# The first projection stage of a short-convolution layer: one written order on all engines in place of the scheduler's

## The chip, the cores and the metric

The kernel runs on one core of a Trainium2 chip. The metric is the device time of one execution in microseconds. Before the change the median of three runs is 918.4 us (918.34 to 922.01). The profiled execution, to which all times of the trace belong, took 920.8 us, with a span of 919.0 us from its first to its last instruction.

In the profile PE is TensorE's matmul, PEld its weight load, DVE is VectorE, ACT is ScalarE, SP is the engine that issues nearly all loads. Each engine takes its instructions in the order in which the program has them.

## The reference

One layer is computed (batch 1, T = 256 positions, model width D = 2048, branch width E = 4096), all in float32:

```python
h = rmsnorm(x, norm_g)
mod = silu(c) @ ada_w + ada_b                # (1, 3*D)
shift, scale, gate = split(mod, 3)
h = h * (1 + scale) + shift                  # 256 x 2048
b_gate, c_gate, v, g = split(h @ w_in, 4)    # w_in: 2048 x 16384, four quarters of 4096
u = causal_depthwise_conv(c_gate * v, conv_w)        # three taps
y = b_gate * u * silu(g)
x = x + gate * (y @ w_out)                   # w_out: 4096 x 2048
out = rmsnorm(x, final_g)
```

## The kernel before, in words

**Products.** Weights and features are float32 and are split into a high part (rounded to the matmul's format) and a low part (the rest). Each product of a 128x128 piece of weights with 256 positions is three matmuls: high by high, high by low, low by high. A load of weights is a block of 128 x 2048 floats (1 MB, tile `raw_s`). ACT casts it into `hi` (line 347), DVE subtracts and writes `lo` (line 348); each of `raw`, `hi` and `lo` has three buffers. Making the two is called parting a block.

**Stages.** After an opening (norm, first features) comes the first w_in stage, whose results are the tiles `mm_s` in PSUM: 16 of the 32 column tiles of every quarter, in four channels of four tiles (names: `acc21` is channel 2, quarter 1). It is done while adaLN's shift and scale are still being summed: of the 16 rows of tiles of w_in (k) only two have features at its start, and more come in pairs. So the stage is done in passes. A pass takes one quarter and one or two channels over those k that have features by then, each channel in a PSUM bank of its own (three exist, tag "mm"). At its end the bank is copied into an accumulator by ACT (line 517, `keep`), or added to it by DVE (line 519); or the bank was seeded with the accumulator beforehand by ACT (line 533) and is only copied out. A bank's share of one block is 24 matmuls. Then the second w_in stage (`mm_b`, the other 16 column tiles) and the last product (`mm_o`) follow.

**adaLN.** A piece is two loads of 128 x 512 floats (tile `at`, 256 KB each, four buffers); DVE multiplies by silu(c) and adds up into `gv` (lines 455 and 457), two instructions a piece. Eight pieces give a pair of k. Then PE transposes (`tp_g`), ACT sums along rows, DVE makes scale and shift (lines 331 to 333), and ACT and DVE write the high and low halves of the pair's features into `hT` (lines 339 to 341). The sums for the residual gate (`at_g`, `gacc`, line 625) belong to the second stage, and the scheduler moves them up into the first where it sees room.

**Mixing.** When a channel has all four quarters, `mixed` multiplies two accumulators (line 570), takes SiLU (571), runs the three-tap filter (ACT line 418, DVE lines 419 and 422), multiplies twice (574, 575), and casts into `y` on ACT (427) and DVE (428), for two column tiles at a time.

**What sets the order.** `plan()` lists the passes, with the pieces to be loaded between blocks and whether a bank is seeded, by a small clock of its own. The program is then written pass by pass, and the framework's scheduler orders each engine's instructions by priority and estimated times; tiles get their buffers in that scheduled order. Three devices hold it: `in_order()` chains all instructions of the opening, `load` chains the first ten loads on SP, `behind` chains the first parts, and `later(GIVE)` puts the sums of adaLN far back in priority. `PACE` says how many pieces go with each of the first ten blocks.

Of the kernel before, what the change touches and what calls it, by code (L numbers as in the profile page):

```python
# [47 lines left out]
WAHEAD = 14.0  # L48
AAHEAD = 6.0


SHARE = 1.5
PACE = (0, 0, 2, 1, 2, 1, 2, 1, 2, 2)


def plan():
# [78 lines left out]
def short_conv_layer(ctx: ExitStack, tc: tile.TileContext, x, c, norm_g, ada_w, ada_b, w_in, conv_w, w_out, final_g, out):  # L135
# [20 lines left out]
    def raw_tile(name):  # L156
        return wpool.tile([P, SLOT], F32, tag="raw", name=name, bufs=3)
# [250 lines left out]
    for k in range(NK0):  # L408
# [1 line left out]
        nc.scalar.copy(hi0[:, c], raw0[:, c])  # L410
        nc.vector.tensor_tensor(out=lo0[:, c], in0=raw0[:, c], in1=hi0[:, c].bitcast(F32), op=ALU.subtract)
        features(k, sh_sc[:, k, 1:2], sh_sc[:, k, 0:1])
    pinned.close()
    pieces0 = [(hi0, lo0)]

    def conv(ct, u, cv):

        nc.scalar.activation(u, cv, AF.Copy, scale=cw[:, 64 + ct : 65 + ct])
        nc.vector.scalar_tensor_tensor(  # L419
            out=u[:, 1:T], in0=cv[:, 0 : T - 1], scalar=cw[:, 32 + ct : 33 + ct], in1=u[:, 1:T], op0=ALU.mult, op1=ALU.add  # L420
        )
        nc.vector.scalar_tensor_tensor(  # L422
            out=u[:, 2:T], in0=cv[:, 0 : T - 2], scalar=cw[:, ct : ct + 1], in1=u[:, 2:T], op0=ALU.mult, op1=ALU.add
        )

    def split_y(dst, y):
        nc.scalar.copy(dst[:, :, 0, :], y)
# [3 lines left out]
    acc = {}  # L431
    sums = {}

    def ada_piece(k0, nk, piece):
        w = nk * P
        kk = ASLOT // (2 * w)
        if piece == 0:
            sums[k0] = adap.tile([P, 2, 2 * P], F32, tag="gv", name="gv")
        gv = sums[k0][:, :, 0:w]
        j = piece * kk  # L440
        at = adap.tile([P, ASLOT], F32, tag="at", name="at", bufs=4)
        at4 = at.rearrange("p (k s f) -> p k s f", k=kk, s=2)
        for s in range(2):
            load(at4[:, :, s, :], adas[:, j : j + kk, s, k0 * P : k0 * P + w])
# [5 lines left out]
    def ada_sums(j, kk, at4, gv):  # L450
        for i in range(kk):
            c_k = silu_c[:, j + i : j + i + 1]
            with behind(ended if first_pieces or j + i == 0 else {}):
                if j + i == 0:
                    nc.vector.tensor_scalar_mul(gv, at4[:, i], c_k)
                else:
                    nc.vector.scalar_tensor_tensor(out=gv, in0=at4[:, i], scalar=c_k, in1=gv, op0=ALU.mult, op1=ALU.add)  # L457

    def ada_done(k0, nk, gv):

        tp = psum.tile([P, 4, P], F32, tag="sm", name="tp_g", bufs=2)
        gs = const.tile([P, 4], F32, tag="gs", name="gs", bufs=2)
        for o in range(2 * nk):
            nc.tensor.transpose(tp[:, o, :], gv[:, o // nk, (o % nk) * P : (o % nk + 1) * P], ident)  # L464
        for o in range(2 * nk):
            nc.scalar.activation(tp[:, o, :], tp[:, o, :], AF.Copy, accum_out=gs[:, o : o + 1])
        modulate(k0, nk, (gs[:, 0:nk], gs[:, nk : 2 * nk]))

    opener = [None]
    first_loads = [None] * 10  # L470

    def load(dst, src):

        ins = nc.sync.dma_start(dst, src)
        if first_loads:
            sp = ins.ins.engine
            tc.add_manual_dep(ins.ins, ended[sp], after, reason="in order")
            ended[sp] = ins.ins.name
            first_loads.pop()

    def product(dst, hi, lo, k, i, begins, left, ends):

        w, h = ((hi, hh_), (hi, hl_), (lo, hh_))[i]
# [34 lines left out]
        else:  # L518
            nc.vector.tensor_tensor(out=acc[ch, q], in0=bank, in1=acc[ch, q], op=ALU.add)

    first_pieces = [None] * 4

    def parts(chs, q, k0, k1, seeds, between):

        w = len(chs) * CT * P
        col = q * E + chs[0] * CT * P
        step = SLOT // w
        first = k0
        banks = []
        for ch, seed in zip(chs, seeds):  # L530
            banks.append(psum.tile([P, CT, T], F32, tag="mm", name="mm_s"))
            if seed:
                nc.scalar.copy(banks[-1], acc[ch, q])
        if pieces0:
            for k in range(NK0):
                chunk_products(banks[0], *pieces0[0], k * CT * P, k, k0, k1, late=True)
            pieces0.clear()
            k0 = NK0
            for some in between:
                for piece in some:  # L540
                    ada_piece(*piece)
        for s0, some in zip(range(k0, k1, step), between):
            sk = min(step, k1 - s0)
            n = sk * w
            raw = raw_tile("raw_s")
            load(
                raw[:, :n].rearrange("p (k f) -> p k f", k=sk),
                w_in[0, s0 * P : (s0 + sk) * P, col : col + w].rearrange("(k p) f -> p k f", p=P),
            )
            with behind(ended if first_pieces else {}, advance=True):  # L550
                hi, lo = split(raw, n)
            del first_pieces[:1]
            for piece in some:
                ada_piece(*piece)
            for j, (bank, seed) in enumerate(zip(banks, seeds)):
                if first == 0:
                    opening_products(bank, hi, lo, w, j * CT * P, s0, sk, k1)
                else:
                    for i in range(sk):
                        chunk_products(bank, hi, lo, i * w + j * CT * P, s0 + i, first, k1, seed)  # L560
        for ch, bank, seed in zip(chs, banks, seeds):
            keep(ch, q, first, bank, seed)

    ys = []

    def mixed(ch):

        for h in range(0, CT, 2):
            cq, vq, gq, bq = (acc[ch, q][:, h : h + 2, :] for q in QUARTERS)
            nc.vector.tensor_tensor(out=cq, in0=cq, in1=vq, op=ALU.mult)  # L570
            nc.scalar.activation(gq, gq, AF.Silu)
            for j in range(2):
                conv(ch * CT + h + j, vq[:, j, :], cq[:, j, :])
            nc.vector.tensor_tensor(out=gq, in0=gq, in1=bq, op=ALU.mult)
            nc.vector.tensor_tensor(out=vq, in0=vq, in1=gq, op=ALU.mult)
            ys.append(slot([P, 2, 2, T], f"y{len(ys)}", F32R))
            split_y(ys[-1], vq)

    whole = [0] * NCH
    for before, *step in plan():  # L580
        for piece in before:
            ada_piece(*piece)
        chs, k1 = step[0], step[3]
        parts(*step)
        for ch in chs:
            whole[ch] += k1 == KT
            if k1 == KT and whole[ch] == 4:
                mixed(ch)
# [208 lines left out]
```

## Time and profile before

| what | value |
|---|---|
| median of three runs | 918.4 us |
| profiled execution | 920.8 us |
| its span | 919.0 us |
| opening, to the first matmul of mm_s | 25.2 us |
| first stage (mm_s) | 25.2 to 388.6 us |
| second stage (mm_b) | 388.6 to 737.3 us |
| last product and end | 737.3 to 919.0 us |

The page's first part gives busy time and share by engine; a busy PE row is modelled at the ends. The chain of waits has the start, the length and the name of each piece of the chain that ended last. A group row ends with the idle time ahead of the group and who ended it. A windows row has the length, the busy time of PE, PEld, DVE, ACT and POOL with the number of instructions, then the granted TensorE clock, the busy share of the DMA engines and their GB/s. A timeline row has start and length, then what and how many, and in brackets the idle time before it.

### The profile page before, as it was taken

To read this page: it belongs to the slowest core of one execution; us is meant where nothing else is said; L and a number is where in the kernel's file an instruction comes from. 1 tells how busy PE (TensorE), PEld (TensorE's weight loads), DVE (VectorE), ACT (ScalarE), POOL (GpSimd) and SP (SyncE) were. 2 spreads that over 40 slices of the span, in tenths; PEclk is the share of its full clock that TensorE was granted. 3 is DMA by queue.
4 is the path that set the end of the run, shared out by engine and by line. 5 is a ranking of instruction groups with operands and counts; after the bars stand their busy time and mean duration, and the time that the engine had idled before them with its cause. 6 is when DMAs were issued, how large, how long until landed. Compare 5 with 4: busy or idle time off the path is not lost.

```text
span 919.0 us, 16211 instructions
## 1 busy us (share of the span) xinstructions
PE 898.6 (98%) x7041; PEld 859.8 (94%) x7041; DVE 629.6 (69%) x603; ACT 453.9 (49%) x431; POOL 2.3 (0%) x9
## 2 busy tenths in 40 slices
PE   7899999999999999999999999999999999999996
PEld 4899999999999999999999999999999988888885
DVE  5698999999886999875545554555454544545882
ACT  6677876554545665543344334433344333443333
POOL 1000000000000000000000000000000000000000
PEclk9999999999999999999999999999999999999999
DMA  9999999999898678676666656666666495566542
GB/s 308 364 375 374 335 358 363 335 375 343 299 322 288 219 275 295 206 243 193 186 196 201 197 184 192 198 203 188 185 191 197 142 356 212 191 204 200 183 137 92
DMA packets 146775, 227.64 MB, mean 248 GB/s; under 512 B 5456, under 2 KB 103808, under 8 KB 146320
## 3 DMA queue, kind: packets, MB, share of 16 engines
q1 hardware_dynamic: 146576, 226.51, 73.4%
q8 instruction: 55, 0.90, 0.4%
q14 instruction: 16, 0.13, 0.0%
q0 software_dynamic: 96, 0.08, 0.0%
q10 hardware_dynamic: 32, 0.01, 0.0%
HBM read 224.49 MB, written 2.10 MB: 247 GB/s over the span
## 4 chain that ended last, share of the span: by engine, by line
PE 91%; DMA 4%; DVE 2%; ACT 1%; issue 1%; SPq 0%; ACTq 0%
PE mm_b L485 38%; PE mm_s L485 34%; PE mm_o L693 6%; PE mm_o L695 6%; PE mm_o L694 6%; DMA at<-in_ada_w_dram 2%; DMA raw_s<-in_sc_w_in_dram 1%; DVE lo L348 1%; ACT hi L347 1%; DMA x<-in_x_dram 1%; DVE acc L419 0%; PE tp_g L464 0%; DVE acc L422 0%; DVE gacc L625 0%; DVE acc L570 0%
## 5 line engine op out<-in xcount | busy, mean ns | idle before, releaser
L485 PE MATMUL mm_b<-hT,hi 128*128 128x256 f32 x2048 | 348.4, 276 | 0.0
L485 PE MATMUL mm_s<-hT,hi 128*128 128x256 f32 x2048 | 338.9, 278 | 7.1 <-ACT acc L517 3.1
L485 PEld LDWEIGHTS mm_s<-hT,hi 128*128 128x128 f32 x2048 | 300.6, 189 | 9.0 <-ACT acc L517 3.5
L485 PEld LDWEIGHTS mm_b<-hT,hi 128*128 128x128 f32 x2048 | 308.2, 188 | 0.0
L485 PE MATMUL mm_b<-hT,lo 128*128 128x256 f32 x1024 | 282.6, 276 | 0.0
L485 PE MATMUL mm_s<-hT,lo 128*128 128x256 f32 x1024 | 262.5, 276 | 0.0
L348 DVE TENSOR_TENSOR lo<-raw,hi 128x2048 fp32r<-128x2048 f32 x64 | 146.7, 2292 | 133.8 <-ACT hi L347 133.8
L347 ACT CAST hi<-raw 128x2048 fp32r<-128x2048 f32 x64 | 122.4, 1913 | 199.1 <-PE mm_b L485 152.4
L485 PEld LDWEIGHTS mm_b<-hT,lo 128*128 128x128 f32 x1024 | 192.2, 188 | 0.1
L485 PEld LDWEIGHTS mm_s<-hT,lo 128*128 128x128 f32 x1024 | 183.0, 188 | 0.0
L347 ACT CAST hi<-raw_s 128x2048 fp32r<-128x2048 f32 (+1 forms) x64 | 121.6, 1900 | 95.4 <-PE mm_s L485 82.8
L348 DVE TENSOR_TENSOR lo<-raw_s,hi 128x2048 fp32r<-128x2048 f32 (+1 forms) x64 | 145.4, 2271 | 17.1 <-ACT hi L347 15.9
L348 DVE TENSOR_TENSOR lo<-raw_o,hi 128x2048 fp32r<-128x2048 f32 x32 | 73.3, 2291 | 64.4 <-ACT hi L347 64.3
L347 ACT CAST hi<-raw_o 128x2048 fp32r<-128x2048 f32 x32 | 61.0, 1907 | 106.8 <-PE mm_o L695 85.3
L694 PE MATMUL mm_o<-lo,y 128*128 128x512 f32 x256 | 99.3, 389 | 0.0
L695 PE MATMUL mm_o<-hi,y 128*128 128x512 f32 x256 | 99.3, 389 | 0.0
L693 PE MATMUL mm_o<-hi,y 128*128 128x512 f32 x256 | 99.3, 389 | 0.0
L457 DVE SCALAR_TENSOR_TENSOR gv<-at,silu_c,gv 128x512 f32<-128x512 f32 x105 | 78.5, 749 | 1.6
L695 PEld LDWEIGHTS mm_o<-hi,y 128*128 128x128 f32 x256 | 48.0, 188 | 10.1
L694 PEld LDWEIGHTS mm_o<-lo,y 128*128 128x128 f32 x256 | 48.0, 188 | 10.0
L693 PEld LDWEIGHTS mm_o<-hi,y 128*128 128x128 f32 x256 | 48.0, 188 | 9.8
L517 ACT COPY acc<-mm_s 128x1024 f32<-128x1024 f32 x43 | 43.3, 1011 | 18.9 <-PE mm_s L485 18.9
(109 smaller groups left out, 377.2 us busy)
## 6 DMA issues: line engine op xcount, KB each, us to landing
raw<-in_sc_w_in_dram SPq DMA_DIRECT2D x64, 1024.0 KB, 5.6
raw_s<-in_sc_w_in_dram SPq DMA_DIRECT2D x63, 1024.0 KB, 7.0
raw_o<-in_sc_w_out_dram SPq DMA_DIRECT2D x32, 1024.0 KB, 5.1
at<-in_ada_w_dram SPq DMA_DIRECT2D x126, 256.0 KB, 7.1
at_g<-in_ada_w_dram SPq DMA_DIRECT2D x32, 512.0 KB, 6.4
x<-in_x_dram SPq DMA_DIRECT2D x4, 512.0 KB, 6.5
big<-in_x_dram SPq DMA_DIRECT2D x2, 1024.0 KB, 7.4
out_dram<-big SPq DMA_DIRECT2D x4, 512.0 KB, 2.9
```

The costliest lines, as they stand in the source:

```text
L347: nc.scalar.copy(hi[:, :n], raw[:, :n])
L348: nc.vector.tensor_tensor(out=lo[:, :n], in0=raw[:, :n], in1=hi[:, :n].bitcast(F32), op=ALU.subtract)
L457: nc.vector.scalar_tensor_tensor(out=gv, in0=at4[:, i], scalar=c_k, in1=gv, op0=ALU.mult, op1=ALU.add)
L485: mm = last_mm[0] = nc.tensor.matmul(dst, w, h[:, k], start=begins and left, stop=ends, skip_group_check=True)
L517: nc.scalar.copy(acc[ch, q], bank)
L693: nc.tensor.matmul(po, yh, hi[:, o], start=opens, stop=False, skip_group_check=True)
L694: nc.tensor.matmul(po, yh, lo[:, o], start=False, stop=False, skip_group_check=True)
L695: nc.tensor.matmul(po, yl, hi[:, o], start=False, stop=ct == NCT - 1, skip_group_check=True)
```

## The change

The first stage is no longer left to the scheduler. `in_order()` now stays open to the end of its last block, so that all that is traced there is chained on each engine in the order written. That order comes from a walk over the blocks with a clock for the loads, PE, DVE and ACT (`clock`, with constants for each kind of work):

- the parts of block b + 2 are written ahead of the products of block b (`part`);
- a piece's sums are written where its estimated landing fits before or after such parts (`sum_some`), or where a pair's features are needed (`get_ready`); the transposes and totals of a pair follow (`turn_sums`, `total_sums`);
- loads are issued as buffers come free (`issue`); a block may go ahead of a piece that has no buffer yet, but not the other way round;
- a bank is opened (and seeded) ahead of the last block of the pass before, the first of two channels is kept between the products of the two, the second at the next block's start;
- mixing is cut into three parts for each two column tiles, written where DVE's clock has room (`mix_some`); what is left over comes after the chain has ended;
- `PACE` is (0, 0, 0, 1, 1, 1, 2, 2, 3, 3) for (0, 0, 2, 1, 2, 1, 2, 1, 2, 2).

The instructions of the stage are the same in number and size. `behind` and `load` are no longer used there.

```diff
-PACE = (0, 0, 2, 1, 2, 1, 2, 1, 2, 2)
+PACE = (0, 0, 0, 1, 1, 1, 2, 2, 3, 3)
...
         features(k, sh_sc[:, k, 1:2], sh_sc[:, k, 0:1])
-    pinned.close()
-    pieces0 = [(hi0, lo0)]
...
-        with later(GIVE):
-            ada_sums(j, kk, at4, gv)
-        if j + kk == KT:
-            ada_done(k0, nk, gv)
...
+    clock = dict(dma=RAW0, pe=FIRST, dve=RAW0 - ISSUE_US, act=FIRST)
...
+    def issue():
+
+        while todo:
+            free = [i for i, (kind, item) in enumerate(todo) if not held(kind, item)]
+            if not free or free[0] and todo[free[0]][0] == "a":
+                return
+            kind, item = todo.pop(free[0])
...
+    def part(b):
...
+        parted[b] = split(raws.pop(b), n)
+        at = spend("act", HI_US * n / SLOT, raws.pop((b, "at")))
+        spend("dve", LO_US * n / SLOT, at)
+        issue()
...
+    def sum_some(end, stall):
+
+        while waiting and waiting[0][2] <= clock["dve"] + stall and max(clock["dve"], waiting[0][2]) + SUM_US <= end:
+            sum_one()
...
+    def total_sums():
+
+        while totals:
+            k0, nk, tp = totals.pop(0)
+            modulate(k0, nk, ada_total(nk, tp))
...
+        def turned():
+            for j, ct in cts:
+                taps(ct, vq[:, j, :], cq[:, j, :])
             nc.vector.tensor_tensor(out=gq, in0=gq, in1=bq, op=ALU.mult)
             nc.vector.tensor_tensor(out=vq, in0=vq, in1=gq, op=ALU.mult)
             ys.append(slot([P, 2, 2, T], f"y{len(ys)}", F32R))
+            nc.scalar.copy(ys[-1][:, :, 0, :], vq)
...
+        total_sums()
+        if b + 2 < N:
+            split_at = max(clock["act"], raws.get((b + 2, "at"), begin)) + HI_US
+            sum_some(split_at + STALL_US, HI_US)
+            part(b + 2)
+        get_ready(s0 + sk)
+        if last and n + 1 in passes:
+            open_bank(n + 1, 0)
+            if len(chs) == 1 and len(passes[n + 1][1]) == 2:
+                open_bank(n + 1, 1)
...
+        sum_some(end + AHEAD_US, STALL_US)
+        mix_some(end + AHEAD_US)
...
+            if j == 0:
+                clock["pe"] = begin + us / len(chs)
+                turn_sums(clock["pe"] - STALL_US)
+                if last and len(chs) == 2:
+                    close_bank(n, 0)
+                    if n + 1 in passes:
+                        open_bank(n + 1, 1)
...
+    pinned.close()
+    close_bank(ended_pass, len(passes[ended_pass][1]) - 1)
+    for us, do in mixing:
+        do()
```

**First place: the loads on SP at the stage's start.** Before (x2 are a piece's two loads):

```order
L474 DMA raw_s_311<-in_sc_w_in_dram 128x2x512
L474 DMA raw_s_345<-in_sc_w_in_dram 128x2x1024
L474 DMA at_352<-in_ada_w_dram 128x2x256 x2
L474 DMA at_357<-in_ada_w_dram 128x2x256 x2
L474 DMA raw_s_416<-in_sc_w_in_dram 128x2x1024
L474 DMA at_422<-in_ada_w_dram 128x2x256 x2
L474 DMA at_487<-in_ada_w_dram 128x2x256 x2
L474 DMA raw_s_481<-in_sc_w_in_dram 128x2x1024
L474 DMA raw_s_551<-in_sc_w_in_dram 128x2x1024
```

Now:

```order
L566 DMA raw_s_283<-in_sc_w_in_dram 128x2x512
L566 DMA raw_s_285<-in_sc_w_in_dram 128x2x1024
L566 DMA raw_s_287<-in_sc_w_in_dram 128x2x1024
L459 DMA at_289<-in_ada_w_dram 128x2x256 x2
L566 DMA raw_s_296<-in_sc_w_in_dram 128x2x1024
L459 DMA at_298<-in_ada_w_dram 128x2x256 x2
L566 DMA raw_s_306<-in_sc_w_in_dram 128x2x1024
```

The third full block (raw_s_481, now raw_s_296) has two loads of pieces ahead of it instead of eight.

**Second place: DVE where the second pair of features (k = 4 and 5) is made.** `gv` are piece sums, `scale` and `shift` the pair's factors, `hT` the features. Before:

```order
L457 SCALAR_TENSOR_TENSOR gv_711<-at_982,silu_c_133,gv_711 128x512 x2
L455 TENSOR_SCALAR gv_1066<-at_1067,silu_c_133 128x512
L348 TENSOR_TENSOR lo_1134<-raw_s_1131,hi_1133 128x2048
L457 SCALAR_TENSOR_TENSOR gv_1066<-at_1067,silu_c_133,gv_1066 128x512
L333 TENSOR_TENSOR shift_172<-gs_988,vec_131 128x2
L331 TENSOR_TENSOR scale_173<-gs_988,vec_131 128x2
L457 SCALAR_TENSOR_TENSOR gv_1066<-at_1072,silu_c_133,gv_1066 128x512
L332 TENSOR_TENSOR scale_173<-scale_173,vec_131 128x2
```

Now:

```order
L364 TENSOR_TENSOR lo_1138<-raw_s_941,hi_1137 128x2048
L474 SCALAR_TENSOR_TENSOR gv_1079<-at_947,silu_c_133,gv_1079 128x512 x2
L474 SCALAR_TENSOR_TENSOR gv_1079<-at_1011,silu_c_133,gv_1079 128x512 x2
L347 TENSOR_TENSOR scale_173<-gs_1206,vec_131 128x2
L348 TENSOR_TENSOR scale_173<-scale_173,vec_131 128x2
L349 TENSOR_TENSOR shift_172<-gs_1206,vec_131 128x2
L356 TENSOR_SCALAR xs1_169<-xs1_169,scale_173,shift_172 128x256
L357 TENSOR_TENSOR hT_167<-xs1_169,hT_167 128x256
```

Two whole pieces (four sums) of the next pair and a low part now stand ahead of the factors. The low part's cast `hi_1137` stands on ACT behind the copy out of bank mm_s_1044. In this region banks change with every block; bank mm_s_975 lies where mm_s_943 was, the bank that PE leaves just before it, and on ACT the copy out of mm_s_943 stands behind the copy out of mm_s_904, the cast `hi_1001` and a seed.

**Third place: mixing of channels 0 and 1, on DVE and ACT.** DVE before, from a low part to the add that empties a bank (line 519):

```order
L348 TENSOR_TENSOR lo_3821<-raw_s_3818,hi_3820 128x2048
L575 TENSOR_TENSOR acc02_410<-acc02_410,acc03_475 128x512 x2
L625 SCALAR_TENSOR_TENSOR gacc_7361<-at_g_7474,silu_c_133,gacc_7361 128x512
L574 TENSOR_TENSOR acc13_477<-acc13_477,acc10_547 128x512 x2
L519 TENSOR_TENSOR acc31_612<-mm_s_3704,acc31_612 128x1024
```

Now, from behind the low part `lo_3672` and a product of two accumulators, to the same add (line 530; line 433 is the filter, 768 the gate sum):

```order
L773 TENSOR_TENSOR gate_s_7241<-gacc_6423,gate_s_7241 128x512
L766 TENSOR_SCALAR gacc_7361<-at_g_7359,silu_c_133 128x512
L433 SCALAR_TENSOR_TENSOR acc02_412<-acc01_336,cw_132,acc02_412 128x255
L768 SCALAR_TENSOR_TENSOR gacc_7361<-at_g_7359,silu_c_133,gacc_7361 128x512
L433 SCALAR_TENSOR_TENSOR acc02_412<-acc01_336,cw_132,acc02_412 128x254
L433 SCALAR_TENSOR_TENSOR acc02_412<-acc01_336,cw_132,acc02_412 128x255
L768 SCALAR_TENSOR_TENSOR gacc_7361<-at_g_7474,silu_c_133,gacc_7361 128x512
L433 SCALAR_TENSOR_TENSOR acc02_412<-acc01_336,cw_132,acc02_412 128x254
L663 TENSOR_TENSOR acc03_482<-acc03_482,acc00_547 128x512
L768 SCALAR_TENSOR_TENSOR gacc_7361<-at_g_7474,silu_c_133,gacc_7361 128x512
L664 TENSOR_TENSOR acc02_412<-acc02_412,acc03_482 128x512
L530 TENSOR_TENSOR acc31_644<-mm_s_3645,acc31_644 128x1024
```

ACT before, around the casts into y:

```order
L347 CAST hi_3874<-raw_s_3872 128x2048
L427 CAST y0_3660<-acc02_410 128x2x256
L427 CAST y1_3673<-acc02_410 128x2x256
L533 COPY mm_s_4036<-acc23_765 128x1024
L347 CAST hi_3928<-raw_s_3926 128x2048
L427 CAST y2_3686<-acc12_412 128x2x256
```

Now, a little later (line 658 is the filter's first row, 635 the seed):

```order
L658 ACTIVATE acc12_439<-acc11_373,cw_132 128x256 x2
L363 CAST hi_3922<-raw_s_3746 128x2048
L666 CAST y2_3934<-acc12_439 128x2x256
L363 CAST hi_3985<-raw_s_3805 128x2048
L635 COPY mm_s_3991<-acc23_763 128x1024
```

The add of acc31 frees the bank that mm_s_3716 takes; the filter and the gate sums now stand ahead of it. On ACT the cast into y2 stands between two blocks' casts and ahead of a seed. On DVE, between `lo_3923` and that cast's input, stand four filter rows and two products. For the cast into y3 there stand twenty filter rows (of channels 1, 2 and 3) and two products behind `lo_4049`.

More of the change, by code (lines that the diff above doesn't have):

```diff
@@ L519, in keep @@
             nc.vector.tensor_tensor(out=acc[ch, q], in0=bank, in1=acc[ch, q], op=ALU.add)
-    first_pieces = [None] * 4
-    def parts(chs, q, k0, k1, seeds, between):
+    flat = []
+    for n, (before, chs, q, k0, k1, seeds, between) in enumerate(plan()):
+        assert not before
         w = len(chs) * CT * P
[L526 to L562, printed above, removed]
@@ L576, in mixed, with low @@
             ys.append(slot([P, 2, 2, T], f"y{len(ys)}", F32R))
[L577 to L588, printed above, removed]
+            nc.scalar.copy(ys[-1][:, :, 0, :], vq)
+        def low():
+            nc.vector.tensor_tensor(out=ys[-1][:, :, 1, :], in0=vq, in1=ys[-1][:, :, 0, :].bitcast(F32), op=ALU.subtract)
```

189 lines of the change are left out of this document (154 added, 35 removed).

## The prediction

> **What bounds the kernel now.** I read the page first (busy shares), then the chain of waits, then the windows and groups of the first stage.
>
> ```profile
> PE 898.6 (98%) x7041; PEld 859.8 (94%) x7041; DVE 629.6 (69%) x603; ACT 453.9 (49%) x431; POOL 2.3 (0%) x9
> ```
>
> TensorE is nearly the whole span, so a change of order can win only what PE waits or loses to its clock. The chain shows where the first stage's PE is released late, and by whom.
>
> ```profile
> 30.23 9.61 DMA raw_s<-in_sc_w_in_dram
> 39.92 1.90 ACT hi L347
> 41.82 0.92 ACT acc L517
> 42.78 22.91 PE mm_s L485 x187
> 65.69 0.44 PE tp_g L464 x4
> ...
> 92.66 1.92 ACT hi L347
> 94.58 0.98 ACT hT L339 x2
> 95.56 0.92 ACT mm_s L533
> 96.52 19.32 PE mm_s L485 x168
> ...
> 204.80 32.70 PE mm_s L485 x288
> ...
> 317.73 2.20 DVE lo L348
> ...
> 321.12 0.60 DVE gate_s L630
> 321.72 1.14 DVE acc L519
> 322.91 65.69 PE mm_s L485 x576
> 388.59 292.40 PE mm_b L485 x2580
> ```
>
> Three releases matter. At 42.8 a block landed late, and the copy out of a finished bank stood behind that block's cast on ACT. At 96.5 the features and a seed copy stood behind a cast on ACT. At 322.9 the add that empties a bank came late on a full DVE. From 388.59 on nothing is touched: 919.0 - 388.6 = 330.4 us stay.
>
> A bank is 24 matmuls: 32.70 / 288 x 24 = 2.72 us. This is the cover that every late row is held against below.
>
> The group rows (first stage) give the durations and the sum of PE's waits.
>
> ```profile
> L485 PE MATMUL mm_s<-hT,hi 128*128 128x256 f32 x2048 | 338.9, 278 | 7.1 <-ACT acc L517 3.1 <-DVE acc L519 2.4 <-ACT mm_s L533 1.5
> L348 DVE TENSOR_TENSOR lo<-raw_s,hi 128x2048 fp32r<-128x2048 f32 (+1 forms) x64 | 145.4, 2271 | 17.1 <-ACT hi L347 15.9 <-DMA at<-in_ada_w_dram 0.3
> L347 ACT CAST hi<-raw_s 128x2048 fp32r<-128x2048 f32 (+1 forms) x64 | 121.6, 1900 | 95.4 <-PE mm_s L485 82.8 <-DMA raw_s<-in_sc_w_in_dram 6.4 <-issue 6.1
> L625 DVE SCALAR_TENSOR_TENSOR gacc<-at_g,silu_c,gacc 128x512 f32<-128x512 f32 x60 | 44.9, 748 | 9.4 <-DMA at_g<-in_ada_w_dram 8.5
> L517 ACT COPY acc<-mm_s 128x1024 f32<-128x1024 f32 x43 | 43.3, 1011 | 18.9 <-PE mm_s L485 18.9
> L519 DVE TENSOR_TENSOR acc<-mm_s,acc 128x1024 f32<-128x1024 f32 x14 | 17.1, 1218 | 1.4 <-PE mm_s L485 1.4
> L339 ACT ACTIVATE hT<-xs,shift,scale 128x256 fp32r<-128x256 f32 x14 | 7.6, 594 | 1.8 <-DVE scale L332 1.8
> L418 ACT ACTIVATE acc<-acc,cw 128x256 f32<-128x256 f32 x16 | 6.8, 498 | 4.2 <-DVE acc L570 4.2
> L419 DVE SCALAR_TENSOR_TENSOR acc<-acc,cw,acc 128x255 f32<-128x255 f32 x16 | 7.3, 477 | 0.0
> L427 ACT CAST y<-acc 128x512 fp32r<-128x512 f32 x4 | 2.5, 625 | 1.8 <-DVE acc L575 1.8
> L574 DVE TENSOR_TENSOR acc<-acc,acc 128x512 f32<-128x512 f32 x6 | 3.9, 682 | 0.0
> ```
>
> The means are from start to end; where one follows another the next starts about 0.09 earlier, which the chain's figures already have (copy 0.92, gacc or gate_s 0.6 to 0.66, a filter row 0.39, a product of two accumulators 0.60).
>
> The timeline and the windows add the slow clock:
>
> ```profile
> 42.78 3.48 PE L485 MATMUL mm_s<-hT,hi 128*128 128x256 f32 x16 [2.46 <-ACT acc L517]
> 47.03 1.99 PE L485 MATMUL mm_s<-hT,hi 128*128 128x256 f32 x16
> 51.36 3.11 DVE L457 SCALAR_TENSOR_TENSOR gv<-at,silu_c,gv 128x512 f32<-128x512 f32 x4
> 40.00:45.00 5.00, 2.54 (x13) 2.33 (x12) 3.15 (x3) 5.00 (x4) 0.00 (x0) 0.73 0.91 335
> 325.00:330.00 5.00, 5.00 (x46) 5.00 (x45) 5.00 (x6) 3.85 (x4) 0.00 (x0) 1.00 1.03 375
> ```
>
> Sixteen matmuls after the long wait took 3.48 instead of 1.99 us: 1.5 us more, at a granted clock of 0.73. So this stage holds 7.1 + 1.5 = **8.6 us** that a better order could win.
>
> **What the change removes.** Loads go ahead of pieces: between the first full block and the third, whose cast ends the opening wait, stood eight piece loads, now two. At the 335 GB/s of the first window row six loads of 262 KB are 4.7 us; PE's two waits there are 3.1 (the group row's ACT acc L517), so I count them as gone, and with it the 1.5 of slow clock. The bounds are 0 and 4.6. The other 4.0 us of waits also leave the sum here, because I count the waits at those places anew. No instruction of the stage is added, dropped or resized; only places change. Hence: -8.6.
>
> **What the written order adds.** Each engine now takes its rows strictly in one order, and the order came from a clock in which PE never waits and ACT never waits for DVE. I walked the new order with the durations above; each term is a chain of rows less the banks that PE has meanwhile.
>
> *Bank mm_s_975.* PE leaves one bank, then has one bank (2.72). ACT has a copy, a cast, a seed and the copy that frees the bank: 0.92 + 1.83 + 0.92 + 1.01 = 4.7. **+2.0**; queued behind is only ACT's next seed.
>
> *Second pair of features.* From the end of bank mm_s_1044 PE has two banks and four transposes, 2.72 x 2 + 0.44 = 5.9. The chain: copy 0.92, cast 1.91, low part 2.20, four piece sums 3.1 (the x4 row), two tiny rows of scale 0.3, feature 0.59: 9.0, so 3.1. The lower half of the features then needs two 0.4 us rows on DVE: 0.8. With some 0.03 us at each hand-over: **+4.1**. Before, the same two rows of scale stood between single piece sums. Two later pairs with the same rows, but more banks in hand, come to 1.6 and 0.6, and the seventh pair's transposes with another to 0.4: **+2.6**.
>
> *Bank mm_s_3716.* From the end of bank mm_s_3586 PE has three banks, 8.2. The chain: cast 1.91, low part 2.20, then on DVE to the add of acc31: three products 1.8, gate_s 0.60, first gate sum 0.40, three more 2.0, four filter rows 1.6, the add 1.22: 11.7, with hand-overs 12.2. **+4.0**. Before, five instructions stood between low part and add.
>
> *Bank mm_s_3991.* When lo_3865 is done PE has 46 matmuls, 5.2. The chain changes engines six times: product 0.69, two filter rows on ACT 0.8, cast 1.91, low part 2.20, four filter rows 1.8, two products 1.4, cast into y2 0.53, cast 1.83, seed 1.02: 12.2. **+7.0**. Here ACT stands at the cast into y2 for 5 us while the next block's cast and the seed, both free to go, are queued behind it, and PE behind them. The chain's start is late itself (lo_3865 behind the cast into y1, 1.3), and the bank's neighbour by 0.4: **+1.7**.
>
> *Cast into y3.* From there PE has six banks, 16.7. The chain: rest of a low part 1.3, product 0.7, filters on ACT 0.8, copy 0.9, cast 1.9, low part 2.2, on DVE twenty filter rows and two products 9.1, cast into y3 0.5, cast 1.9: 19.3, so 2.6; the block's own low part follows with 2.2: **+4.8**.
>
> Sum: 2.0 + 4.1 + 2.6 + 4.0 + 7.0 + 1.7 + 4.8 = **26.2**. It can be smaller, since a wait at one place gives the other engines time for the next (I carried that through, but only as well as the durations hold): lower bound half, 13. It can be larger by late landings: before, gate sums waited 8.5 us for loads (L625 row), and in a strict order that passes on to the adds; upper bound +8.
>
> *Clock.* A long PE wait cost 1.5 more at 42.8 and nothing at 322.9 (granted clock 1.00 in the window row after it). Four of the new waits are as long: bounds 0 and 6, I take the middle, **+3**, since the trace has one case of each.
>
> [...]
>
> **Sum.** The profiled execution took 920.8 (span 919.0 and 1.8 around it): 920.8 - 8.6 + 26.2 + 3 = 941.4. The median of the runs is 918.4, that is 2.4 below it: **939.0 us**, 2.2% slower.
>
> **Rivals.**
>
> *Covered after all (faster).* The new order runs parts two loads ahead. If ACT and DVE in truth enter each chain one block (two banks, 5.4 us) earlier than I count, 4.1, 4.0, 2.0 and 4.8 vanish and 7.0 + 1.7 shrink to some 3; with 8.6 won: 918.4 - 8.6 + 3 = 913. It decides wherever a cast can start before PE has left an older block. For it: DVE's low parts wait just 17.1 us in the stage. Against it: ACT's casts wait 82.8 us for PE (L347 row), that is, for the buffers, and they are no more than before. 9%.
>
> *Waits overlap.* The late chains share their lateness and half of the sum goes: 918.4 - 8.6 + 13 = 923, at the border of slower. For it: an engine that PE keeps waiting for goes on working meanwhile. Against it: the chains start anew from PE's leaving a bank. 12%, of it 4% within 0.5%.
>
> *Clock and landings (slower still).* All four waits pay 1.5, and 8 us of late gate loads go through: 939 + 3 + 8 = 950. For it the 8.5 us; against it that most of these loads are issued long ahead. 9%.
>
> *No effect.* The scheduler might have kept its own order: the rows of the new program show that it did not. Under 1%.
>
> **How the numbers follow.** Forecast (928 to 948) 70%, overlap 12%, slower still 9%, faster 9%. About 0.5% is what a measurement of this kernel tells from no change. Slower by more: 70 + 8 + 9 = 87%; within: 4%; faster: 9%. The range leaves out the faster case and the far end of the slowest: 926 to 948.
>
> **What would show it.** Right: PE's wait before mm_s in the new group row near 27 instead of 7.1, released by features, the add of accumulators and seed copies; ACT's casts into y waiting some 20 us or more for DVE instead of 1.8; no PE wait and full clock from 27 to 80; mm_b starting near 408 instead of 388.6. Wrong: PE's wait below 10 with mm_b starting before 388, or the loss lying in the opening, or after the first stage, whose 330.4 us must stand.

## The result, and the profile after

The changed kernel takes **951.6 us** (median of six runs, 947.4 to 954.0) against 919.2 for the kernel before on the same chip: a ratio of **1.035, 95% interval 1.032 to 1.038**, or 32.4 us slower. The forecast was 939.0 with a range of 926 to 948: the direction is right, the size is not.

The profiled execution took 953.9 us (span 952.1), 2.3 above the median. The first stage now runs from 25.3 to 421.5, which is 396.2 us in place of 363.3. All else stands: 421.5 to 952.1 is 330.6, against 330.4. The second stage starts at 421.5, forecast near 408. So all of the loss lies in the stage that was rewritten.

Section 1 of the page after:

```profile
PE 911.2 (96%) x7041; PEld 871.5 (92%) x7041; DVE 635.1 (67%) x603; ACT 453.7 (48%) x431; POOL 2.3 (0%) x9
```

As many instructions on every engine as before. ACT is no busier (453.7, before 453.9) and DVE hardly (635.1, before 629.6); PE's busy time grew by 12.6 with the same 7041 matmuls, so some of them ran slower.

The groups of the first stage, idle time at the end of each row:

```profile
L496 PE MATMUL mm_s<-hT,hi 128*128 128x256 f32 x2040 | 348.1, 283 | 23.1 <-DVE acc L530 8.7 <-ACT mm_s L635 7.2 <-ACT hT L355 3.3
L355 ACT ACTIVATE hT<-xs,shift,scale 128x256 fp32r<-128x256 f32 x14 | 7.7, 595 | 20.4 <-DVE shift L349 20.4
L666 ACT CAST y<-acc 128x512 fp32r<-128x512 f32 x4 | 2.5, 619 | 27.9 <-DVE acc L664 27.9
L768 DVE SCALAR_TENSOR_TENSOR gacc<-at_g,silu_c,gacc 128x512 f32<-128x512 f32 x60 | 45.0, 750 | 9.8 <-DMA at_g<-in_ada_w_dram 8.8
L766 DVE TENSOR_SCALAR gacc<-at_g,silu_c 128x512 f32<-128x512 f32 x4 | 1.9, 487 | 6.9 <-DMA at_g<-in_ada_w_dram 6.9
```

PE waits 23.1 us where it waited 7.1. ACT stands 27.9 at the casts into `y` (before 1.8) and 20.4 at the features (before 1.8). Each row's own time is that of before: the work is the same, and it stands in queues. The last two rows are the gate's sums, which are not part of the written order; together they wait 15.7 us for their loads.

The chain of waits, at five places (dots stand for pieces left out; `issue` pieces of under 0.1 us are left out too):

```profile
87.19 1.03 ACT acc L528
88.26 4.27 PE mm_s L496 x23
...
106.92 0.61 ACT hT L355
...
108.48 18.84 PE mm_s L496 x143
...
326.27 0.76 DVE gacc L768
...
329.30 2.22 DVE lo L364
331.57 0.75 DVE gacc L768
332.32 0.07 DVE acc L530
...
336.76 7.21 DMA at_g<-in_ada_w_dram
344.00 0.49 DVE gacc L766
...
349.35 0.07 ACT y L666
...
380.50 1.89 ACT hi L363
382.40 0.92 ACT mm_s L635
383.36 17.98 PE mm_s L496 x143
...
405.24 16.40 PE mm_s L496 x142
421.65 3.40 PE mm_b L496 x30
```

At 88 PE gets its bank only after ACT's copy; at 107 the features come late; at 326 to 332 an add that empties a bank stands on DVE behind sums of the gate, and at 337 to 344 a sum of the gate waits for its load ahead of the filter and the next such add; at 383 a seed comes late. The load of the first of these sums held DVE for 3.90 us (timeline):

```profile
326.27 3.12 DVE L768 SCALAR_TENSOR_TENSOR gacc<-at_g,silu_c,gacc 128x512 f32<-128x512 f32 x4 [3.90 <-DMA at_g<-in_ada_w_dram]
```

The windows show what each wait brings with it (the number behind POOL's is the granted clock):

```profile
30.00:85.00 55.00, 55.00 (x472) 55.00 (x471) 46.03 (x46) 41.45 (x42) 0.00 (x0) 1.00 0.99 352
90.00:95.00 5.00, 5.00 (x33) 5.00 (x33) 3.37 (x5) 2.45 (x2) 0.00 (x0) 0.71 1.05 383
110.00:115.00 5.00, 5.00 (x31) 5.00 (x31) 4.89 (x5) 1.98 (x3) 0.00 (x0) 0.66 0.53 150
335.00:340.00 5.00, 5.00 (x47) 5.00 (x46) 4.96 (x5) 3.56 (x3) 0.00 (x0) 1.00 0.87 298
350.00:355.00 5.00, 4.55 (x21) 4.55 (x22) 4.84 (x6) 3.21 (x3) 0.00 (x0) 0.50 0.64 202
```

From 30 to 85 us there is no wait and full clock. In the windows behind the waits at 88, 108 and 350 the clock is 0.5 to 0.71: in the first two PE is busy all the time and does 33 and 31 matmuls in 5 us where it otherwise does 43 to 47. Behind the wait of 3.2 us at 333.5 it stays at 1.00.

**The account.** I counted the starts of neighbouring matmuls of the stage in both traces (0.113 us apart at full clock, 0.213 at half; a wait counts from the start that was due). Before: 8.4 us of waits and one run of 12 half-speed matmuls (1.3). After: 30.5 us of waits and six runs with 13 to 23, together 101 (10.1). That is 22.2 more waits and 8.8 more slow clock; the other 1.9 of the 32.9 are many small steps.

### The profile page after: what moved, and what is told of

Read it like the earlier page. It is cut to its first block, busy times and chain, and to the rows that moved or that the text cites. A ratio compares the mean times of both kernels' runs of the same rounds, so it can differ in the third digit from the quotient of the medians.

```text
span 952.1 us, 16220 instructions
## 1 busy us (share of the span) xinstructions
PE 911.2 (96%) x7041; PEld 871.5 (92%) x7041; DVE 635.1 (67%) x603; ACT 453.7 (48%) x431; POOL 2.3 (0%) x9
## 4 chain that ended last, share of the span: by engine, by line
PE 71%; DVE 11%; DMA 9%; issue 4%; ACT 4%; SPq 0%; ACTq 0%; DVEq 0%
PE mm_b L496 37%; PE mm_s L496 16%; PE mm_o L837 6%; PE mm_o L836 6%; PE mm_o L838 6%; DMA at_g<-in_ada_w_dram 5%; DVE lo L364 4%; DVE gv L474 3%; ACT hi L363 3%; DMA at<-in_ada_w_dram 3%; DVE gacc L768 2%; DMA x<-in_x_dram 1%; DMA raw_s<-in_sc_w_in_dram 1%; DVE acc L433 0%; ACT mm_s L635 0%
## 5 line engine op out<-in xcount | busy, mean ns | idle before, releaser
L496 PE MATMUL mm_s<-hT,hi 128*128 128x256 f32 x2048 | 349.5, 283 | 23.1 <-DVE acc L530 8.7
L496 PEld LDWEIGHTS mm_s<-hT,hi 128*128 128x128 f32 x2048 | 309.2, 193 | 25.5 <-DVE acc L530 9.3
L496 PE MATMUL mm_s<-hT,lo 128*128 128x256 f32 x1024 | 267.9, 281 | 1.8 <-DVE lo L364 1.8
L496 PEld LDWEIGHTS mm_s<-hT,lo 128*128 128x128 f32 x1024 | 188.4, 193 | 2.0 <-DVE lo L364 2.0
L528 ACT COPY acc<-mm_s 128x1024 f32<-128x1024 f32 x43 | 43.5, 1015 | 21.3 <-PE mm_s L496 21.2
```

The costliest lines, as they stand in the source:

```text
L496: mm = last_mm[0] = nc.tensor.matmul(dst, w, h[:, k], start=begins and left, stop=ends, skip_group_check=True)
L528: nc.scalar.copy(acc[ch, q], bank)
```

## The experiments

The theory: PE waits at a few places where the written order puts rows that must wait ahead of rows that are free to go, and each wait is paid twice, once as itself and once as half-speed matmuls behind it. All ratios are to the kernel before, run on the same chip in the same session.

### The late third: mixing left to the scheduler

```diff
         sum_some(end + AHEAD_US, STALL_US)
-        mix_some(end + AHEAD_US)
```

All mixing is then written after the chain has ended.

> The whole written order stays except the mixing of finished chunks (products of accumulators, filter rows, casts into y), which is left to the scheduler again, after the last block's rows in the program. Theory (the late third of the loss is the mixing in the written order): the waits at 350.5 (5.9 + 0.3), 383.4 (5.8 + 0.3), 402.9 and 405.2 (1.6 + 2.0) go, 15.9 us, and the 23 and 13 half-speed matmuls behind the first two with them, 3.6: 951.6 - 19.5 = 932, PE's wait before mm_s some 10 to 12 us in the group row. The wait of 3.2 at 333.5 stays or goes with the gate sums' places. Rival (the gate sums' late loads hold DVE, whatever the mixing does): the adds stay late, at most 6 us are won, 945 or more. Rival (the slow clock has a cause of its own): the waits go and the half-speed matmuls stay, 936.

Measured: **928.7 us**, ratio 1.009 [1.006, 1.012]. The waits at 350 to 405 are gone, and their half-speed matmuls too (mean granted clock 0.992, in the changed kernel 0.984). In the waits (us in total, times, longest) ACT's casts into `y` fall from 27.9 to 3.7:

```profile
ACT y L666 <- DVE acc L664: 3.7, 3, 1.6
```

So more than two thirds of the loss is the mixing in the written order. The rival that the gate's loads alone made it late falls. Still there, beside the waits of the first 110 us, are waits of 2.4 us at 241, 2.5 at 328 and 2.4 at 336.

### The late third: gate sums held out of the stage

```diff
-        with later(GIVE):
+        with later(GIVE), behind(ended):
             gate_sums(dc, j, at3)
```

> The changed kernel with the gate's sums (the rows of gacc, outside the written order) held behind the last row of the written order on DVE and SP, so that none of them stands in the first stage. Theory (in the last third, written rows and gate sums that wait for their loads add up on DVE): the 3.2 at 333.5 goes, the 5.9 at 350.5 shrinks to under 2 and its half-speed matmuls go, the 5.8 at 383.4 and the 3.6 at 403 to 405, which are chains of mixing through ACT, stay: 951.6 - 3.2 - 4.2 - 2.3 = 942, a little less won if gate sums are then late behind the later stage. Rival (the mixing alone is late): at most 2 us are won, 950. Rival (gate sums are the whole of the late third): 951.6 - 21 = 931.

Measured: **950.9**, ratio 1.034 [1.031, 1.037], no gain. But the first stage ends at 405.6 instead of 421.5: the waits of 2.8 at 246 and 3.2 at 333 are gone, and the 5.9 at 350 is 1.8. The chains of mixing through ACT stay (6.6 and 3.3). Nearly all that was won is lost again in the second stage, 360.7 us long instead of 348.7, where PE had waited for nothing; the waits there:

```profile
PE mm_b L496 <- DVE lo L364: 6.6, 8, 2.5
```

The theory's three places are right and its time is wrong: it allowed little for the second stage. What follows: the gate's sums are a second cause in the late third, yet they must stand somewhere, and both causes act together. With the mixing out of the written order and one more bank seeded (the whole-stage experiment below) the same sums do little harm where they are: they wait 2.8 us for their loads and PE's waits come to 1.9. Why their loads then land in time isn't shown. With the mixing out alone they still waited 11.5 us.

### The late third: mixing in the written order, one step for a block

```diff
-            nc.scalar.copy(ys[-1][:, :, 0, :], vq)
+            casts.append((ys[-1], vq))
...
     def mix_some(end):
-        while mixing and clock["dve"] + mixing[0][0] <= end:
+        cast_some()
+        if mixing and clock["dve"] + mixing[0][0] <= end:
```

`cast_some` writes the casts that are waiting in `casts`.

> The changed kernel with the mixing still in the written order, but at most one of its steps for a block of w_in, and each cast into y moved a block later on ACT. Theory (ACT stands at a cast into y while the next cast and seed are queued behind it, because up to three steps are written in one place): the waits at 350 (5.9), 383 (5.8) and 403 to 405 (3.6) become one of about 4 near 400, with 23 and 13 half-speed matmuls fewer; ACT's casts into y wait under 10 us for DVE instead of 28: 951.6 - 11 - 3 = 937. Rival (DVE is simply full there and the same work is late wherever it stands): the add and the casts stay late, 948 to 952. The waits of the first half (2.2, 3.5, 2.8) stay in both.

Measured: **937.3**, ratio 1.018 [1.014, 1.022]. In the profiled execution, at 933.6 the fastest of its four, the late third has waits of 1.3, 1.3 and 4.4 in place of 3.2, 5.9, 5.8 and 3.6. ACT's stand at the casts is shorter, though not as short as I expected:

```profile
ACT y L680 <- DVE acc L664: 17.9, 5, 7.1
```

DVE had as much to do as in the changed kernel (634.0 us busy, against 635.1), so it isn't simply full: of 19 us of waits in the late third 12 went with no more than a change of the rows' places.

### The first half: one more seeded bank

```diff
+    flat = [(n, chs, q, k0, k1, [True, True] if n == 10 else seeds, w, s0, sk, some) for n, chs, q, k0, k1, seeds, w, s0, sk, some in flat]
     N = len(flat)
```

The eleventh pass (n == 10) had [True, False].

> The changed kernel with one flag: the second bank of the eleventh pass (mm_s_975) is seeded too, so ACT's copy claims its bank in its place in the written order, and the add that ended it on DVE becomes a copy on ACT. Theory (an unseeded bank is claimed only when PE gets to it, while the seeds of the pass behind it have already taken the free ones): the wait of 2.2 at 88 goes, and with the add gone and two piece sums in place of four ahead of scale also the 3.5 + 0.8 + 0.3 at 108 for the second pair of features, with the 16 and 21 half-speed matmuls behind them: 951.6 - 6.8 - 3.7 = 941, the late third unchanged within 1.5. Rival (the features wait for their pieces, not for a place on DVE): only 2.2 and 1.6 go, 948. Rival (the wait at 88 is ACT's load and a further seed makes it worse): 951 or more.

Measured: **938.6**, ratio 1.019 [1.016, 1.022]. Both waits are gone, at 88 and at 107, and from 25 to 188 us PE waits for nothing:

```profile
L496 PE MATMUL mm_s<-hT,hi 128*128 128x256 f32 x2048 | 346.1, 281 | 13.8 <-ACT mm_s L636 6.3 <-DVE acc L530 5.3 <-ACT hi L363 2.3
```

No wait for a copy (ACT acc L528) or for features (ACT hT L355) is among the causes any more. My reading of the program, which the run supports but doesn't show by itself: a bank that is not seeded gets its place in PSUM when PE opens it; by then the seeds of the next pass, written ahead on ACT, had taken both free places, and mm_s_975 was left with the one that PE was about to leave. With a seed of its own it claims a place in turn. The add on DVE that this saves also moved the sums: in the trace two instead of four stand ahead of the second pair's `scale`, and they are done 1.6 us before it can start. The edit does both at once, so what each is worth alone isn't shown.

### The opening alone: the first 14 blocks in written order

```diff
+        if b == 14:
+            pinned.close()
         us = sk * len(chs) * CT * 3 * PRODUCT_US
...
-    pinned.close()
```

> The written order ends in front of the fifteenth block (about 100 us into the span); from there the scheduler places everything, as before the change, while plan, loads and pieces stay the changed ones. Theory (the opening is a gain, the later chains are the loss): no PE wait to 85 us, one of about 2.2 at 88 with some 16 half-speed matmuls behind it, and behind 100 us about what the kernel before had (1.7 at 96.5, 2.7 at 322.9 or less): 919.2 - 8.4 - 1.3 + 2.2 + 1.6 + at most 3 = 913 to 916. Rival (the opening's gain is lost because features come later, so the waits only move): 919 to 922, with a PE wait of 3 us or more between 95 and 110. Rival (the whole loss is in how loads and pieces are issued): over 935.

Measured: **924.7**, ratio 1.004 [1.003, 1.006]. My theory said 913 to 916 and missed; the rival with a wait of over 3 us between 95 and 110 is right in the place, though its time (919 to 922) was short too:

```profile
PE mm_s L496 <- ACT acc L528: 3.9, 2, 2.1
PE mm_s L496 <- DVE hT L357: 3.5, 1, 3.5
```

The bank at 86 (2.2 us from start to start) and the features at 107 take back what the opening wins, even though the scheduler places the features again; the other wait of the first row, 2.0, is at 303, in the part that the scheduler orders.

### The opening's table alone, in the kernel before

```diff
-PACE = (0, 0, 2, 1, 2, 1, 2, 1, 2, 2)
+PACE = (0, 0, 0, 1, 1, 1, 2, 2, 3, 3)
```

> The kernel before with nothing but the table PACE of the change, the scheduler placing everything as before. Theory (fewer pieces at the start end the opening wait and make the first features' sums late): the waits of 0.8 and 2.6 at 37 to 43 go with 12 half-speed matmuls, and waits of some 1.8 and 3.8 for features or their bank come near 70 to 76: 918 to 924, no gain. Rival (the loads' order alone is the gain of the opening): 919.2 - 3.7 - 1.3 = 914.

Measured: **925.5**, ratio 1.004 [1.002, 1.006]. As the theory has it: no wait before 71 us, then 1.8 and 3.7 for the first pair of features. The loads' order alone moves the wait from blocks to features and makes it longer.

```profile
PE mm_s L485 <- DVE hT L341: 3.5, 1, 3.5
```

### Both repairs: 20 blocks in written order with the seed

The two diffs above (`b == 20`, and the seed).

> The seed of the run before, and the written order ends in front of the twenty-first block (some 135 us into the span), from where the scheduler places everything again. Theory (the changed plan and loads are a gain, and all of the loss stands in three places of the written order: the bank of 975, the second features, the late third): no PE wait over 1 us from 27 us to 300 and at most one of about 2 behind it, stage of mm_s to mm_b 352 to 356 instead of 363 before: 919.2 - 363.3 + 354 = 910 (907 to 914), faster than both. Rival (the scheduler's part loses as much as with the first 14 blocks written, where waits of 2.0, 1.0 and 0.7 stood behind 300): 915 to 918. Rival (the early loads cost later what they win): 919 or more.

Measured: **912.0**, ratio **0.990 [0.987, 0.993]**: faster than both kernels, by 1.0% than the one before. The stage takes 354.4 us, 8.9 less than before:

```profile
L496 PE MATMUL mm_s<-hT,hi 128*128 128x256 f32 x2048 | 336.4, 277 | 0.0
```

PE's wait in this group is 0.0 (before 7.1, after 23.1). So the opening's gain is there to be had, if its price at the bank and the features isn't paid.

### Both repairs in the whole stage

The written order to the end of the stage, without `mix_some` and with the seed.

> The written order to the end of the stage, with the mixing left to the scheduler and the second bank of the eleventh pass seeded. Theory (these two cover nearly all of the loss): against the run with the mixing left out alone (928.7), 2.2 + 4.5 of waits and some 20 half-speed matmuls go: 928.7 - 6.7 - 2 = 920, and with the 2.4 at 241 gone as well (other places of the sums) 916. Rival (the seed only moves the wait to the next seeded bank): 926 or more.

Measured: **913.4**, ratio 0.992 [0.989, 0.995], better than I expected. A written order for the whole stage is no loss in itself: with the places of the mixing and of one bank mended, it wins nearly what the 20 blocks win.

### The old table in the repaired kernel

The kernel with 20 blocks and the seed, with `PACE` as it was before.

> The fastest version so far (911.96: written order to the twentieth block, second bank of the eleventh pass seeded) with the old table PACE, so that eight pieces' loads stand again between the first full block and the third, all else the same. Theory (the change of PACE is a gain in itself once the later chains are mended): waits of some 0.5 and 1.3 between 34 and 42 come back, and since the sums then fall on other places 1.1 and 0.8 at the second features: 3.7 and up to 1.5 of slow clock: 916 to 917. Rival (the old table would have been as good in a written order, the opening wait was the scheduler's): 912. Rival (earlier pieces help the features): under 911.

Measured: **916.7**, ratio 0.995 [0.993, 0.997]. The waits are 0.5 and 1.2 at 37 and 41 and 1.1 and 0.8 at 100, as expected, and none is followed by half-speed matmuls (mean granted clock 0.998): half a per cent (0.995 against 0.990) is the table's own gain in this kernel.

### The clock: waits filled in the changed kernel

```diff
+            fill(FILL.get((b, j), 0))
             if b == 0:
```

`fill(n)` writes n matmuls of 128x256 into a spare tile of the transposes' kind in PSUM.

> The changed kernel with 85 matmuls of 128x256 more, which compute nothing that is used: 17 ahead of bank mm_s_975, 28 ahead of the products on the second pair's upper half, 40 ahead of bank mm_s_3716, all placed where PE waits anyway (2.2, 3.5 and 5.9 us there). Nothing else moves. Theory (each wait costs its length and then 13 to 23 matmuls at half speed): the waits are filled, the 16 + 21 + 23 half-speed matmuls behind them run at full speed, 60 x 0.1 = 6 us are won by doing more work: 945.5, with granted clock near 1.00 in 85 to 115 and 350 to 355. Rival (the slow clock has a cause of its own, such as the load on the array): nothing is won, 951 to 953, half-speed matmuls stay. Rival (the forecast's size, 3 us for all waits): 1.5 to 2 are won, 950.

Measured: **950.1**, ratio 1.031 [1.028, 1.034] against 1.035: not to be told apart in time. In the trace the three waits are filled and their 60 half-speed matmuls are gone, but runs of 12 and 16 came behind two other waits that had none in the profile after, and the wait at 380 grew by 1.6 (mean granted clock 0.987, in the changed kernel 0.984). A kernel with a dozen waits is too uneven for this question, so I made a cleaner pair.

### The clock: six bare stops, and six filled ones

Into the 912.0 us kernel:

```diff
...
+        idle_product(to[:, 0:T])
+        for _ in range(STOPS[b]):
+            nc.scalar.copy(to[:, 0:T], to[:, 0:T])
+        if b in IDLES:
...
+            for _ in range(IDLES[b]):
+                idle_product(by[:, 0:T])
+        idle_product(to[:, 0:T])
```

`to` and `by` are two tiles of the transposes' kind; `IDLES` is empty in the kernel with bare stops.

> The same fastest version with six stops put into PE's order ahead of the 5th, 7th, 10th, 12th, 16th and 18th block: PE makes one product that nobody uses, ACT copies it in place once or five times, and PE's next product waits for that. By the rows of the traces the stops are about 3.3, 4.2, 3.5, 5.3, 3.1 and 4.2 us, 23.6 in all, and nothing else gets late. Theory (nearly every wait of this length is followed by 12 to 23 half-speed matmuls): 912 + 23.6 + 6 x 1.7 = 946. Rival (a third to a half of them is, as the forecast's 3 us for four waits has it): 912 + 23.6 + 6 x 0.75 = 940. Rival (no price): 935.5. [...]

> The kernel with six stops, and in each stop 25 to 43 matmuls of 128x256 that nobody uses, so that PE works through all but the last 0.3 to 0.5 us of each; the stops themselves and all other rows are the same. Theory (the price is that of PE standing still): 912 + 23.6 + about 0.5 = 936, that is 10 below the kernel with the bare stops, with granted clock 1.00 throughout. Rival (the price comes with the matmuls, or is none): the same time as with bare stops.

Measured: **951.4** with bare stops (1.033 [1.029, 1.036]), **941.1** with filled ones (1.021 [1.018, 1.024]). Both are 5 above what I expected, most of it because the stops came out longer (26.9 us with the step behind each, not 23.6); the difference is 10.3 us, as the theory has it. The second kernel does 186 matmuls more and is 1.1% faster. One stop (ahead of the 18th block), bare, in the timeline (start, length of the group, idle time in brackets) and the window around it:

```profile
152.34 0.58 PE L635 MATMUL tp_stop<-hT 128*128 128x256 f32 x1 [4.61 <-ACT tp_stop L644]
150.00:155.00 5.00, 2.66 (x12) 2.66 (x13) 4.24 (x5) 2.16 (x6) 0.00 (x0) 0.67 1.03 350
```

and the window of the same stop when filled:

```profile
145.00:150.00 5.00, 5.00 (x46) 5.00 (x45) 1.61 (x3) 0.00 (x0) 0.00 (x0) 1.00 1.04 357
```

In the bare kernel all six stops (3.2 to 5.9 us) are followed by 13 to 27 half-speed matmuls, 120 in all (mean granted clock 0.980). In the filled one (0.997) a single run of 13 is left, behind the one stop whose products ran out 2.2 us early. So in this pair the price is that of standing still: 10.3 / 6 = 1.7 us for a stop at the least, since one stop still pays in the filled kernel; the 120 matmuls of the bare one, 0.1 us each, come to 2.0.

## Why the prediction was right in kind and wrong in size

**What holds.** The first stage alone changed; the remaining 330.4 stand (330.6). The opening wins what was counted: no PE wait from 25 to 85 us and full clock from 30 on, and the repaired kernel shows that the 8.6 can be had (the stage is 8.9 shorter). PE's wait in the group row, forecast near 27, is 23.1 there, and ACT's casts into `y` wait 27.9, forecast 20 or more. The places of the waits were all named but one.

**Term by term** (waits from start to start): the bank of mm_s_975, 2.0 forecast, 2.2 measured; the second pair of features 4.1 and 4.5; the two later pairs 1.6 and 0.6, measured 1.5 and 0.4. These were walked row by row and came out within 0.4. In the late third the walk was less good: bank 3991 with its late start 8.7, measured 6.1; the cast into y3 4.8, measured 3.6, 3.8 us less together. That each wait gave the engines time for the next, as the text said it might, is the likely reason; no run shows it.

**First step that failed: late landings were a bound and not a term.** Three waits came out longer or were not foreseen: the seventh pair's transposes 2.8 instead of 0.4, bank 3586 at 333 with 3.2 instead of nothing, bank 3716 with 6.2 instead of 4.0. That is 7.8 us, against an "upper bound +8" for gate sums that wait for their loads, which the sum took as zero. The trace of after shows it at the first of the three (DVE, timeline):

```profile
243.25 0.49 DVE L766 TENSOR_SCALAR gacc<-at_g,silu_c 128x512 f32<-128x512 f32 x1 [2.65 <-DMA at_g<-in_ada_w_dram]
243.66 0.75 DVE L474 SCALAR_TENSOR_TENSOR gv<-at,silu_c,gv 128x512 f32<-128x512 f32 x1
244.98 0.75 DVE L474 SCALAR_TENSOR_TENSOR gv<-at,silu_c,gv 128x512 f32<-128x512 f32 x1
```

A gate sum waits 2.65 us for its load, and behind it stand the last sums of the pair for which PE waits. At the other two places DVE stands 3.90 (shown above) and 1.57 us for such a load, 8.1 in all. With the gate sums held back, two of these waits vanished and the third fell to 1.8; that run takes away the sums' own time too, so the part of the late landing rests on the trace. The late landings and the shorter late third partly cancel: waits altogether 19.1 us more forecast (26.2 - 7.1), 22.2 measured.

**Second step that failed, and the larger: the clock, +3, measured 10.1.** The price of one wait (1.5) was nearly right: the six runs of slow matmuls cost 1.7 each on average, and the stops 1.7 to 2.0. Wrong was how many pay. I took the middle between all and none, "since the trace has one case of each", and counted only the four waits of 4 us and more. Three of these paid (21, 23 and 13 matmuls, 5.7 us); the one for y3, which came in two parts of 1.6 and 2.0, paid nothing. The 2.2 and the 2.8 paid as well (16 and 15, 3.1 us), and one run of 13 (1.3) stands at the stage's first matmuls (granted clock 0.69 from 25 to 30 us, 1.00 in the trace of before); its cause stays open. What decides whether a wait of 2 to some 3 us pays is not shown; the last section has the cases.

**The rivals.** *Clock and landings slower still* (950, 9%) is what happened, by its two own mechanisms; that its time came within 2 us is in part luck, since the clock took more than it gave it (10.1, not 6) and the late third less. *Covered after all* falls: the casts entered no chain earlier. *Waits overlap* falls in size: 3.8 us of the late third, not half of the sum. *No effect* falls.

One slip in the working: six banks are 16.3 us by its own 2.72, not 16.7, which makes the cast into y3 5.2 instead of 4.8.

## What to carry to other kernels

A written order must be checked at each row that waits for another engine or for a load: what is free to go and stands behind it? Here a cast into an output held back the next block's cast and a seed, and unpinned sums that waited for loads held back pinned rows. By these runs I would price a PE wait of 3 us or more at its length and some 1.7 us on top (an estimate from the six runs of slow matmuls, 10.1 us, and the six stops, 10.3), a wait of 2 to 3 at that or nothing; which of the two it will be is not shown ahead of a run. And, as far as the one seed shows it, a tile that is claimed at first use can lose its buffer to one that was written later but is filled ahead.

## What the runs showed of the hardware beside that

I had not expected how uneven the price of a wait is. These are the waits of PE over 0.5 us in the first stage of the traces of before and after, from start to start, each with the granted clock in a window that reaches behind it:

| kernel | wait ends at | wait, us | granted clock (window) | half-speed matmuls behind it |
|---|---|---|---|---|
| before | 37.2 | 0.8 | 1.00 (35 to 40) | none |
| before | 42.8 | 2.6 | 0.73 (40 to 45) | 12 |
| before | 96.5 | 1.7 | 1.00 (95 to 100) | none |
| before | 322.9 | 2.7 | 1.00 (325 to 330) | none |
| after | 88.3 | 2.2 | 0.71 (90 to 95) | 16 |
| after | 107.6 and 108.5 | 3.5 and 0.8 | 0.66 (110 to 115) | 21 |
| after | 167.7 | 1.5 | 1.00 (165 to 170) | none |
| after | 245.8 | 2.8 | 0.66 (245 to 250) | 15 |
| after | 333.5 | 3.2 | 1.00 (335 to 340) | none |
| after | 350.5 | 5.9 | 0.50 (350 to 355) | 23 |
| after | 383.4 | 5.8 | 0.85 (385 to 390) | 13 |
| after | 402.9 | 1.6 | 1.00 (400 to 405) | none |
| after | 405.2 | 2.0 | 1.00 (405 to 410) | none |

Leaving out the pair at 108, the five from 0.8 to 2.0 us paid nothing, of the four from 2.2 to 2.8 three paid, and of the three from 3.2 up two; the pair paid too. The six bare stops of 3.2 to 5.9 us all paid, the four waits of 0.5 to 1.2 with the old table did not (mean granted clocks 0.980 and 0.998).

The wait of 2.2 us at mm_s_975 comes again in other kernels. The changed kernel paid 16 matmuls for it. The kernel with the first 14 blocks in written order paid nothing: in its chain of waits 96 matmuls follow in 11.22 us, 0.117 each. Nor did the kernel with the mixing left to the scheduler. PE stands about 2.05 us in the changed kernel's windows (first: 3.42 - 1.37) and as long in those of the latter (second: 1.54 and 0.51), with a granted clock of 0.50 behind it in the first and 1.00 in the second:

```profile
86.11:89.53 3.42, 1.37 (x11) 1.27 (x11) 3.11 (x3) 3.02 (x4) 0.00 (x0) 1.00 1.06 387
89.53:92.94 3.41, 3.41 (x18) 3.41 (x17) 2.28 (x4) 0.39 (x1) 0.00 (x0) 0.50 1.06 387
```

```profile
81.93:85.34 3.41, 1.87 (x17) 1.67 (x15) 2.87 (x4) 3.41 (x4) 0.00 (x0) 1.00 1.10 378
85.34:88.75 3.41, 2.90 (x25) 2.90 (x26) 3.30 (x5) 1.38 (x2) 0.00 (x0) 1.00 1.04 384
88.75:92.17 3.42, 3.42 (x33) 3.42 (x32) 3.08 (x3) 3.35 (x3) 0.00 (x0) 1.00 1.04 389
```

What parts these cases is not shown, nor why the 2.6 at 42.8 paid and the 2.7 at 322.9 did not, or why the 3.2 at 333.5 paid nothing. So I take the price of a wait of 2 to some 3 us as a matter of luck for whoever writes the order.
